# First query weights loaded third and used behind the second feature tile

## The chip, the cores and the metric

One core of a Trainium2 chip (trn2). The time is that of one launch in microseconds of device time, from three runs of each kernel. Engines, as the profile names them: PE (TensorE, matmuls), PEld (its weight loads), DVE (VectorE), ACT (ScalarE), POOL (GpSimd), SP (SyncE, which here issues nearly all loads). Each engine works through its own instructions in the order in which they stand; a semaphore holds an instruction until another engine, or a transfer, has got far enough.

## What is computed

A two-layer encoder on 512 frames of width 1024, in float32. Layer 0 is multi-head latent attention with a chunk mask and a SwiGLU feed-forward, layer 1 chunked attention over shared keys and values with another feed-forward. The change lies in the first 100 us, in the entry of layer 0:

```python
h = rms_norm(x, attn_pre_g[0])
a = h @ w_a                                   # 1024 -> 384 + 256 + 64
cq, ckv, kr = split(a, [384, 640])
q = (rms_norm(cq, g_q) @ w_uq)                # 8 heads: 128 plain + 64 rotary columns
kv = (rms_norm(ckv, g_kv) @ w_ukv)            # 8 heads: 128 key + 128 value columns
s = (q_nope k_nope^T + rope(q_rope) rope(k_rope)^T) * scale    # block-causal mask, softmax, p @ v, w_o
```

## The kernel before

Everything is kept transposed: features on 128 partitions, the 512 frames along the free side, so x is eight tiles `x[0]` to `x[7]` of 128x512. Each float32 operand is split into a high half, rounded to the format that PE multiplies, and the low rest: ACT writes the high half (`whi` of weights L144, `xh` of features L148, with the gain), DVE the rest (`wlo` L145, `xl` L149). `mm3` (L358) makes one product of three matmuls, high by high, high by low, low by high, each with 512 columns.

The norm's factor is not applied to x: the projection runs on x times the gain, and the factor of each frame is multiplied in later. So beside the projection ACT squares each x tile (L425, L428) and DVE adds the squares (L429, class `Sum`).

Weights come through `Feed`: a plan of tiles, added in order (L728 to L758); `load` issues a tile's DMA into one of 5 raw buffers, `split` makes `whi` and `wlo` in one of 3 buffers each, `next` hands out the next split tile, `ahead` splits one more early. The names in the profile: `in_w_akv` are the eight tiles of the 256 latent key/value and 64 rotary key columns (384 columns, one feature tile each), `in_w_aq` four tiles of the 384 query-latent columns (768 columns, two feature tiles each), then `in_w_uv` (values), `in_w_uqr` (rotary query), `in_w_qk` (a head's query and key).

`load_x` (L762) issues x tile k and then weight tile k. From the third on, POOL first writes one element of the new tile from an element of a tile two places earlier (L767, L286). That copy waits for the earlier tile's landing, and the DMA waits for the copy, so only some loads are under way at a time.

The loop L790 to L802 does, for each of the eight feature tiles: split the weights, split x, nine matmuls into three PSUM banks `b1` (three output tiles of three terms), issue the next loads, split the next weights ahead, square x. The four `in_w_aq` tiles follow in `proj` (L363), eighteen matmuls each into three banks `b2`, after the loop. Between its pieces (`some(rest, n)`) stand the sums of squares (`tot`, L438), the two factors by a power on POOL (L456), and their spreading over partitions on PE (`bc`, L473). Then the key/value latent is multiplied with its factor (L863) and split (`ckh`, `ckl`), and come the values `va` (L894), the rotary query (L908), the heads (L930) and attention, whose scores `sc` (L1013 to L1017) DVE turns into `p` (L498). The eight PSUM banks are four of tag `mm`, two `s`, two `t`: a matmul into a fresh bank waits until the bank's last reader is done.

The order on each engine is made by a scheduler from priorities (program order, which `first(n)` moves n places forward) and from its own estimate of durations; `issue_after` keeps an instruction behind another.

Of the kernel before, what the change touches and what calls it, by code (L numbers as in the profile page):

```python
# [11 lines left out]
F32R = mybir.dt.float32r  # L12
I32 = mybir.dt.int32
AF = mybir.ActivationFunctionType
OP = mybir.AluOpType
# [3 lines left out]
D, S, P = 1024, 512, 128  # L19
KT = D // P  # L20
# [48 lines left out]
def trunk(ctx: ExitStack, tc: tile.TileContext, a, out):  # L69
    nc = tc.nc  # L70
    V = nc.vector
# [10 lines left out]
    def name_(n):  # L82
        uid[0] += 1
        return f"{n}_{uid[0]}"

    def U(dt=F32, name="u"):
        return up.tile([P, S], dt, tag="u", name=name_(name), bufs=NU)
# [4 lines left out]
    def bank(tag="mm", name="b"):  # L92
        return ps.tile([P, S], F32, tag=tag, name=name_(name), bufs={"mm": 4, "s": 2, "t": 2}[tag])
# [29 lines left out]
    def g(n, k):  # L123
        return gains[:, n * KT + k:n * KT + k + 1]

    G_APRE, G_APOST, G_FPRE, G_FPOST = (0, 1), (2, 3), (4, 5), (6, 7)
# [8 lines left out]
    @contextmanager  # L135
    def first(n):

        tc.cur_priority -= n
        yield
        tc.cur_priority += n  # L140


    def split(dst_hi, dst_lo, src):
        return (nc.scalar.copy(dst_hi, src),  # L144
                V.tensor_tensor(dst_lo, src, dst_hi.bitcast(F32), op=OP.subtract))  # L145

    def split_scaled(dst_hi, dst_lo, src, col):
        return (nc.scalar.activation(dst_hi, src, AF.Copy, scale=col),  # L148
                V.scalar_tensor_tensor(dst_lo, src, col, dst_hi.bitcast(F32), op0=OP.mult, op1=OP.subtract))  # L149
# [202 lines left out]
    feed = Feed()  # L352
# [5 lines left out]
    def mm3(o, l, r, start, stop):  # L358
        nc.tensor.matmul(o, l[0], r[0], start=start, stop=False)  # L359
        nc.tensor.matmul(o, l[0], r[1], start=False, stop=False)  # L360
        nc.tensor.matmul(o, l[1], r[0], start=False, stop=stop)  # L361

    def proj(n_out, n_k, kc, rhs, banks, ahead=True):  # L363

        cols = n_out * P
        for c in range(0, n_k, kc):
            m = min(kc, n_k - c)
            w = feed.next(m * cols, ahead)
            for kk in range(m):
                if kk == 1:  # L370
                    feed.ahead()
                while len(rhs) <= c + kk:
                    yield False
                for j in range(n_out):
                    mm3(banks[j], w(kk * cols + j * P, P), rhs[c + kk], c + kk == 0, c + kk == n_k - 1)
                    yield True
# [82 lines left out]
    def rstd_of_scaled(ss, n, r0):  # L459

        v = small("v2")
        V.tensor_tensor(v, ss, r0, op=OP.mult)
        V.tensor_tensor(v, v, r0, op=OP.mult)
        r = rstd(v, n)
        o = small("r2")
        V.tensor_tensor(o, r, r0, op=OP.mult)
        return o
# [157 lines left out]
    def out_proj(rhs, n_k, post, have, n_last, late):  # L625
# [9 lines left out]
        for m in groups[:-n_last]:  # L635
            b = [bank() for _ in range(m)]
            weave(proj(m, n_k, KC[m], rhs, b))
            done.extend(b)
# [88 lines left out]

    for k in range(KT):  # L728
        feed.add(a["w_akv"][k], 384)
    for k in range(KT // 2):  # L730
        feed.add(a["w_aq"][k], 768)
    feed.add(a["w_uv"][0], 1024)
    feed.add(a["w_uqr"][0], 768)
# [26 lines left out]
    x = []  # L760

    def load_x():  # L762

        k = len(x)
        t = U(name="x")
        if k > 1:
            nc.gpsimd.tensor_copy(t[:1, :1], x[k - 2][:1, :1])  # L767
            feed.gate = feed.raw[k - 2]
        nc.sync.dma_start(t, a["x"][:, k])
        x.append(t)  # L770
        feed.load(k)
        feed.gate = None

    for k in range(4):
# [2 lines left out]
    def load_positions():  # L777
        for c in range(NQT):
            nc.sync.dma_start(pos_i[32 * c:32 * c + 32],
                            bass.AP(tensor=a["positions"].tensor, offset=a["positions"].offset + c * P,  # L780
                                    ap=[[0, 32], [1, P]]))
        nc.sync.dma_start(inv, a["inv_freq"])
# [4 lines left out]

    xs, sx = [], Sum()
    b1 = [bank() for _ in range(3)]
    for k in range(KT):  # L790
        h, l = U(F32R, "xh"), U(F32R, "xl")
        w = feed.next(384, False)
        feed.behind[k + 1] = split_scaled(h, l, x[k], g(G_APRE[0], k))
        xs.append((h, l))
        for j in range(3):
            mm3(b1[j], w(j * P, P), xs[k], k == 0, k == KT - 1)
        if len(x) < KT:
            load_x()
        feed.ahead()
        if k == 3:  # L800
            load_positions()
        sx.add(x[k])  # L802
    b2 = [bank("s"), bank("s"), bank()]
    rest = proj(3, KT, 2, xs, b2)
    skv = Sum()
    for j in range(2):
        skv.add(b1[j])
    ckv = []
# [8 lines left out]
    with first(100):  # L817
        rkv = rstd_of_scaled(ss, KVL, r0)
# [40 lines left out]
    rkv = spread(rkv)  # L859
    r0b = spread_sb(r0)  # L860
    cks = []
    for j in range(2):
        V.tensor_tensor(ckv[j], ckv[j], rkv, op=OP.mult)  # L863
        h, l = U(F32R, "ckh"), U(F32R, "ckl")
        feed.behind[13] = feed.behind[14] = split(h, l, ckv[j])
        cks.append((h, l))
    kr = U(name="kr")
    V.tensor_tensor(kr, b1[2], r0b, op=OP.mult)
# [5 lines left out]
    for j in range(3):  # L874
        h, l = U(F32R, "cqh"), U(F32R, "cql")
# [612 lines left out]
    x, sx = post.x, post.split  # L1488
    xs = sx.xs
# [20 lines left out]
    rest = v_half(0)  # L1510
# [137 lines left out]
    for kc in range(4):  # L1648
        w = feed.next(1024)
# [99 lines left out]
```

## Time and profile before

| | |
|---|---|
| runs | 1121.03, 1118.68, 1120.24 us; median 1120.24 |
| profiled execution | 1120.65 us, of which the span from first to last instruction is 1118.9 us |
| PE busy | 1102.8 us (99%) |
| DVE, ACT busy | 931.9 us (83%), 685.4 us (61%) |
| POOL busy | 70.4 us (6%) |
| granted TensorE clock, mean over the span | 0.999 |
| DMA | 150.85 MB, mean 135 GB/s |

PE is busy almost throughout, so a microsecond is won or lost only where PE waits. A matmul row's duration runs past the start of the next row, since matmuls are pipelined; the distance from start to start is what one costs.

### The profile page before, as it was taken

The numbers are of one execution on the slowest core, as the hardware profiler recorded it, in microseconds if no ns is written. First come the engines' busy times: TensorE is split into PE (matmuls) and PEld (weight loads), VectorE is DVE, ScalarE is ACT, GpSimd is POOL, SyncE is SP. The second block draws the span as 40 slices with busy tenths as digits, with TensorE's granted clock in tenths as the row PEclk, the third lists the DMA queues.
The fourth block names the chain that finished last, engine by engine and source line by source line (L and its number), as shares of the span: only waits on it lengthen the run. The fifth ranks groups of instructions, "written<-read, shape, count | busy, mean of one in ns | idle before, by whom it ended". The sixth has DMA issues, their size and how long they took to land.

```text
span 1118.9 us, 18985 instructions
## 1 busy us (share of the span) xinstructions
PE 1102.8 (99%) x6973; PEld 984.2 (88%) x6973; DVE 931.9 (83%) x1671; ACT 685.4 (61%) x1339; POOL 70.4 (6%) x106
## 2 busy tenths in 40 slices
PE   9999999999999999999999999999999999999997
PEld 6888889999999998888788888888999999998885
DVE  7788737999989889978858878657999899889977
ACT  6476637755555556668536777666755555566675
POOL 2200000000000002400100000000000000002402
PEclk9999999999999999999999999999999999999999
DMA  7333125323332448871456665534422322449923
GB/s 237 113 109 87 65 74 208 133 83 106 94 115 95 131 161 248 139 216 35 173 151 169 154 181 146 152 118 166 147 80 95 123 86 96 141 169 291 171 56 76
DMA packets 62991, 150.85 MB, mean 135 GB/s; under 512 B 8433, under 2 KB 10225, under 8 KB 62897
## 3 DMA queue, kind: packets, MB, share of 16 engines
q1 hardware_dynamic: 55552, 136.61, 38.6%
q0 software_dynamic: 6912, 12.59, 6.8%
q8 instruction: 55, 0.90, 0.3%
q10 hardware_dynamic: 432, 0.44, 0.1%
q14 instruction: 40, 0.32, 0.1%
HBM read 119.52 MB, written 9.63 MB: 115 GB/s over the span
## 4 chain that ended last, share of the span: by engine, by line
PE 84%; DVE 7%; DMA 3%; ACT 3%; issue 2%; POOL 1%; SPq 0%; POOLq 0%; DVEq 0%; ACTq 0%
PE al L1453 16%; PE b L359 10%; PE b L360 10%; PE b L361 10%; PE be L1453 8%; PE al L1203 8%; PE ga L1453 4%; PE be L1203 4%; PE de L1203 3%; PE ga L1203 3%; PE pt L512 2%; DVE wlo L145 2%; ACT whi L144 1%; DVE raw L174 1%; DMA raw<-in_w_pair 1%
## 5 line engine op out<-in xcount | busy, mean ns | idle before, releaser
L144 ACT CAST whi<-raw 128x1024 fp32r<-128x1024 f32 (+3 forms) x224 | 225.3, 1007 | 208.4 <-PE al L1453 74.0
L145 DVE TENSOR_TENSOR wlo<-raw,whi 128x1024 fp32r<-128x1024 f32 (+3 forms) x224 | 261.3, 1168 | 55.9 <-ACT whi L144 54.1
L1453 PE MATMUL al<-th,whi 128*128 128x256 f32 x432 | 122.8, 284 | 0.8 <-DVE ut L1465 0.8
L1453 PE MATMUL al<-th,wlo 128*128 128x256 f32 x432 | 121.1, 280 | 0.0
L1453 PE MATMUL al<-tl,whi 128*128 128x256 f32 x432 | 120.9, 280 | 0.0
L359 PE MATMUL b<-xh,whi 128*128 128x512 f32 (+1 forms) x304 | 117.3, 387 | 0.0
L360 PE MATMUL b<-xl,whi 128*128 128x512 f32 (+1 forms) x304 | 112.7, 371 | 0.2 <-DVE xl L149 0.2
L361 PE MATMUL b<-xh,wlo 128*128 128x512 f32 (+1 forms) x304 | 112.5, 370 | 0.0
L174 DVE TENSOR_TENSOR raw<-raw,raw 128x1024 f32<-128x1024 f32 x72 | 86.7, 1220 | 1.3 <-DMA raw<-in_w_pair 1.2
L1453 PEld LDWEIGHTS al<-th,whi 128*128 128x128 f32 x432 | 81.2, 188 | 3.2 <-DVE ut L1465 1.2
L1453 PEld LDWEIGHTS al<-th,wlo 128*128 128x128 f32 x432 | 81.3, 188 | 0.1
L1453 PEld LDWEIGHTS al<-tl,whi 128*128 128x128 f32 x432 | 81.3, 188 | 0.0
L500 ACT ACTIVATE p<-p,mn 128x128 f32<-128x128 f32 (+1 forms) x96 | 54.0, 562 | 39.5 <-DVE mn L498 38.4
L145 DVE TENSOR_TENSOR ptl<-pt,pth 128x128 fp32r<-128x128 f32 (+1 forms) x96 | 46.7, 486 | 29.4 <-ACT pth L144 23.7
L145 DVE TENSOR_TENSOR wlo<-wd,whi 128x512 fp32r<-128x512 f32 x86 | 56.7, 689 | 14.4 <-ACT whi L144 14.2
L361 PEld LDWEIGHTS b<-xh,wlo 128*128 128x128 f32 x304 | 57.5, 189 | 9.5
L144 ACT CAST whi<-wd 128x512 fp32r<-128x512 f32 x86 | 50.0, 618 | 25.5 <-PE al L1203 10.6
L359 PEld LDWEIGHTS b<-xh,whi 128*128 128x128 f32 x304 | 57.8, 190 | 7.1 <-ACT xh L148 0.7
L360 PEld LDWEIGHTS b<-xl,whi 128*128 128x128 f32 x304 | 57.8, 190 | 7.1 <-DVE xl L149 1.1
L144 ACT CAST pth<-pt 128x128 fp32r<-128x128 f32 (+1 forms) x96 | 40.3, 420 | 26.6 <-PE pt L512 25.7
L1203 PE MATMUL al<-whi,ph 128*128 128x512 f32 x132 | 51.8, 392 | 0.0
L1203 PE MATMUL al<-whi,pl 128*128 128x512 f32 x132 | 51.5, 390 | 0.0
(309 smaller groups left out, 3267.8 us busy)
## 6 DMA issues: line engine op xcount, KB each, us to landing
raw<-in_w_pair SPq DMA_DIRECT2D x72, 512.0 KB, 3.6
wd<-in_w_down SPq DMA_DIRECT2D x54, 256.0 KB, 5.7
raw<-in_w_o SPq DMA_DIRECT2D x16, 512.0 KB, 3.6
raw<-in_w_gu SPq DMA_DIRECT2D x16, 512.0 KB, 3.9
raw<-in_w_down SPq DMA_DIRECT2D x16, 512.0 KB, 4.3
raw<-in_w_qkb SPq DMA_DIRECT2D x16, 512.0 KB, 3.7
wd<-in_w_down POOLq DMA_DIRECT2D x22, 256.0 KB, 5.9
wd<-raw POOLq DMA_DIRECT2D x22, 256.0 KB, 4.4
```

The lines of the kernel that those rows point to most:

```text
L144: return (nc.scalar.copy(dst_hi, src), V.tensor_tensor(dst_lo, src, dst_hi.bitcast(F32), op=OP.subtract))
L145: V.tensor_tensor(dst_lo, src, dst_hi.bitcast(F32), op=OP.subtract))
L174: V.tensor_tensor(t, x, y, op=OP.add)
L359: nc.tensor.matmul(o, l[0], r[0], start=start, stop=False)
L360: nc.tensor.matmul(o, l[0], r[1], start=False, stop=False)
L361: nc.tensor.matmul(o, l[1], r[0], start=False, stop=stop)
L500: nc.scalar.activation(p[:, :n], p[:, :n], AF.Exp, bias=mn[:, :1], scale=-1.0, accum_out=self.sums[:, qt:qt + 1])
L512: nc.tensor.transpose(t[:, kt * P:(kt + 1) * P], p[:, kt * P:(kt + 1) * P], ident)
L1203: nc.tensor.matmul(to[e], l[c], r[d], start=j < 4 and k == 0 and n == 0, stop=k == NF // 2 - 1 and n == 2, skip_group_check=True)
L1453: nc.tensor.matmul(o, l[c], r[d], start=first_ and n == 0, stop=k == K2 - 1 and n == 2, skip_group_check=True)
```

## The change

The plan puts the first `in_w_aq` tile third, behind the second `in_w_akv` tile. `load_x` issues its DMA ahead of the third x tile, and later weight tiles one call later by index. In the loop x is split ahead of the weights (for all but the first tile), the matmuls of the first two feature tiles go term by term over the three banks instead of bank by bank, squares of x are taken one tile later, and behind the second feature tile the early query tile is used with both: eighteen matmuls, which `proj` then leaves out (`begun=2`). The multiplication and split of the key/value latent get priority 100.

```diff
--- before.py
+++ after.py
@@ -360,10 +360,10 @@
         nc.tensor.matmul(o, l[0], r[1], start=False, stop=False)
         nc.tensor.matmul(o, l[1], r[0], start=False, stop=stop)
 
-    def proj(n_out, n_k, kc, rhs, banks, ahead=True):
+    def proj(n_out, n_k, kc, rhs, banks, ahead=True, begun=0):
 
         cols = n_out * P
-        for c in range(0, n_k, kc):
+        for c in range(begun, n_k, kc):
             m = min(kc, n_k - c)
             w = feed.next(m * cols, ahead)
             for kk in range(m):
@@ -727,7 +727,9 @@
 
     for k in range(KT):
         feed.add(a["w_akv"][k], 384)
-    for k in range(KT // 2):
+        if k == 1:
+            feed.add(a["w_aq"][0], 768)
+    for k in range(1, KT // 2):
         feed.add(a["w_aq"][k], 768)
     feed.add(a["w_uv"][0], 1024)
     feed.add(a["w_uqr"][0], 768)
@@ -762,13 +764,16 @@
     def load_x():
 
         k = len(x)
+        if k == 2:
+            feed.gate = feed.raw[0]
+            feed.load(2)
         t = U(name="x")
         if k > 1:
             nc.gpsimd.tensor_copy(t[:1, :1], x[k - 2][:1, :1])
-            feed.gate = feed.raw[k - 2]
+            feed.gate = feed.raw[k - 1 if k > 3 else k - 2]
         nc.sync.dma_start(t, a["x"][:, k])
         x.append(t)
-        feed.load(k)
+        feed.load(k if k < 2 else k + 1)
         feed.gate = None
 
     for k in range(4):
@@ -787,21 +792,40 @@
 
     xs, sx = [], Sum()
     b1 = [bank() for _ in range(3)]
+    b2 = [bank("s"), bank("s"), bank()]
     for k in range(KT):
         h, l = U(F32R, "xh"), U(F32R, "xl")
-        w = feed.next(384, False)
-        feed.behind[k + 1] = split_scaled(h, l, x[k], g(G_APRE[0], k))
+        w = None if k else feed.next(384, False)
+        s = split_scaled(h, l, x[k], g(G_APRE[0], k))
+        if k:
+            feed.behind[feed.pos] = s
+            w = feed.next(384, False)
         xs.append((h, l))
-        for j in range(3):
-            mm3(b1[j], w(j * P, P), xs[k], k == 0, k == KT - 1)
+        if k < 2:
+
+            for n, (c, d) in enumerate(((0, 0), (0, 1), (1, 0)) if k else ((0, 0), (1, 0), (0, 1))):
+                for j in range(3):
+                    nc.tensor.matmul(b1[j], w(j * P, P)[c], xs[k][d], start=k + n == 0, stop=False)
+        else:
+            for j in range(3):
+                mm3(b1[j], w(j * P, P), xs[k], False, k == KT - 1)
         if len(x) < KT:
             load_x()
-        feed.ahead()
         if k == 3:
             load_positions()
-        sx.add(x[k])
-    b2 = [bank("s"), bank("s"), bank()]
-    rest = proj(3, KT, 2, xs, b2)
+        if k:
+            with ExitStack() as order:
+                for i in s if k < 3 else ():
+                    order.enter_context(tc.issue_after(i.ins))
+                sx.add(x[k - 1])
+        if k == 1:
+            w = feed.next(768, False)
+            for i in range(2):
+                for j in range(3):
+                    mm3(b2[j], w(i * 384 + j * P, P), xs[i], not i, False)
+    feed.ahead()
+    sx.add(x[-1])
+    rest = proj(3, KT, 2, xs, b2, begun=2)
     skv = Sum()
     for j in range(2):
         skv.add(b1[j])
@@ -860,9 +884,10 @@
     r0b = spread_sb(r0)
     cks = []
     for j in range(2):
-        V.tensor_tensor(ckv[j], ckv[j], rkv, op=OP.mult)
-        h, l = U(F32R, "ckh"), U(F32R, "ckl")
-        feed.behind[13] = feed.behind[14] = split(h, l, ckv[j])
+        with first(100):
+            V.tensor_tensor(ckv[j], ckv[j], rkv, op=OP.mult)
+            h, l = U(F32R, "ckh"), U(F32R, "ckl")
+            feed.behind[13] = feed.behind[14] = split(h, l, ckv[j])
         cks.append((h, l))
     kr = U(name="kr")
     V.tensor_tensor(kr, b1[2], r0b, op=OP.mult)
```

PE, the nine matmuls of the first feature tile and the first of the second (`b_` are the PSUM banks, the first x tile's halves are `xh_125`, `xl_126` before and `xh_131`, `xl_132` now). Before:

```order
L359 MATMUL b_122<-xh_125,whi_127 128x512
L360 MATMUL b_122<-xl_126,whi_127 128x512
L361 MATMUL b_122<-xh_125,wlo_128 128x512
L359 MATMUL b_123<-xh_125,whi_127 128x512
L360 MATMUL b_123<-xl_126,whi_127 128x512
L361 MATMUL b_123<-xh_125,wlo_128 128x512
L359 MATMUL b_124<-xh_125,whi_127 128x512
L360 MATMUL b_124<-xl_126,whi_127 128x512
L361 MATMUL b_124<-xh_125,wlo_128 128x512
L359 MATMUL b_122<-xh_154,whi_148 128x512
```

Now:

```order
L808 MATMUL b_125<-xh_131,whi_133 128x512
L808 MATMUL b_126<-xh_131,whi_133 128x512
L808 MATMUL b_127<-xh_131,whi_133 128x512
L808 MATMUL b_125<-xh_131,wlo_134 128x512
L808 MATMUL b_126<-xh_131,wlo_134 128x512
L808 MATMUL b_127<-xh_131,wlo_134 128x512
L808 MATMUL b_125<-xl_132,whi_133 128x512
L808 MATMUL b_126<-xl_132,whi_133 128x512
L808 MATMUL b_127<-xl_132,whi_133 128x512
L808 MATMUL b_125<-xh_154,whi_158 128x512
```

The low half of x was read by the second matmul and is now read by the seventh; the low half of the weights moved from the third to the fourth.

DVE, from the end of the first rotary product to the split of the first value tile of the second value half (`ra`, `rb` rotary products of the query, `rl` their low half, `r_` the query norm's factor from POOL, `va` values; L917 is L942 now, L915 and L916 are L940 and L941). Before:

```order
L917 TENSOR_TENSOR ra_643<-ra_643,rb_644 128x512
L452 TENSOR_SCALAR v_610<-v_131_607 128x4
L145 TENSOR_TENSOR wlo_772<-raw_695,whi_771 128x640
L466 TENSOR_TENSOR r_134_614<-r_612,r_356 128x4
L145 TENSOR_TENSOR rl_649<-ra_643,rh_648 128x512
L981 TENSOR_SCALAR nsq<-r_134_614 128x4
L145 TENSOR_TENSOR va_543<-b_720,va_543 128x512
```

Now:

```order
L452 TENSOR_SCALAR v_611<-v_131_608 128x4
L145 TENSOR_TENSOR wlo_733<-raw_626,whi_732 128x640
L466 TENSOR_TENSOR r_134_615<-r_613,r_381 128x4
L942 TENSOR_TENSOR ra_644<-ra_644,rb_645 128x512
L1006 TENSOR_SCALAR nsq<-r_134_615 128x4
L145 TENSOR_TENSOR rl_650<-ra_644,rh_649 128x512
L940 TENSOR_TENSOR ra_653<-b_618,sin_431 128x512
L941 TENSOR_TENSOR rb_654<-b_619,cos_432 128x512
L145 TENSOR_TENSOR wlo_773<-raw_696,whi_772 128x640
L145 TENSOR_TENSOR va_544<-b_721,va_544 128x512
```

The add into `ra` stands behind POOL's factor now, and two more rotary products and the weight split stand between `rl` and the value split.

ACT, around the key of the first head (`kh_706` before, `kh_707` now; `whi` 768 columns wide is the second rotary weight tile). Before:

```order
L144 CAST kh_706<-b_710 128x512
L144 CAST whi_838<-raw_729 128x640
L144 CAST qh_778<-b_762 128x512
L144 CAST whi_928<-raw_769 128x768
L144 CAST kh_780<-b_784 128x512
```

Now:

```order
L144 CAST whi_839<-raw_730 128x640
L144 CAST qh_705<-b_689 128x512
L144 CAST whi_929<-raw_770 128x768
L144 CAST kh_707<-b_711 128x512
L144 CAST qh_779<-b_763 128x512
L144 CAST kh_781<-b_785 128x512
```

The first head's key stood ahead of both weight casts and now stands behind the 768-column one; that cast takes the buffer of the second head's weights, and so waits until PE has read these for the last time, in both kernels.

## Rows read from the trace of the kernel before

**Rows 1.** The page's busy time of each engine: us, share, instructions.

```profile
PE 1102.8 (99%) x6973; PEld 984.2 (88%) x6973; DVE 931.9 (83%) x1671; ACT 685.4 (61%) x1339; POOL 70.4 (6%) x106
```

**Rows 2.** Stages: start:end length, busy us (instructions) per engine, granted clock, DMA share, GB/s.

```profile
5.00:11.00 6.00, 5.76 (x20) 4.08 (x20) 4.09 (x7) 4.04 (x8) 1.99 (x7) 1.00 0.78 224
...
31.50:60.00 28.50, 28.25 (x130) 22.68 (x128) 22.23 (x41) 14.75 (x26) 4.87 (x4) 1.00 0.40 112
60.00:75.00 15.00, 15.00 (x82) 12.87 (x83) 13.42 (x30) 13.30 (x29) 0.00 (x0) 1.00 0.49 136
```

**Rows 3.** PE in order of time: start, us, line, tiles, [idle before].

```profile
4.97 0.79 PE L359 MATMUL b<-xh,whi 128*128 128x512 f32 x1
5.76 0.79 PE L360 MATMUL b<-xl,whi 128*128 128x512 f32 x1
6.35 0.63 PE L361 MATMUL b<-xh,wlo 128*128 128x512 f32 x1
6.78 0.50 PE L359 MATMUL b<-xh,whi 128*128 128x512 f32 x1
7.12 0.39 PE L360 MATMUL b<-xl,whi 128*128 128x512 f32 x1
...
8.91 0.50 PE L360 MATMUL b<-xl,whi 128*128 128x512 f32 x1 [0.24 <-DVE xl L149]
...
10.85 0.40 PE L359 MATMUL b<-xh,whi 128*128 128x512 f32 x1
```

**Rows 4.** POOL, ACT, DVE at the start, in order of time.

```profile
5.95 0.17 POOL L767 COPY x<-x 1x1 f32<-1x1 f32 x1 [1.26 <-DMA x<-in_x]
...
6.41 0.51 ACT L144 CAST whi<-raw 128x384 fp32r<-128x384 f32 x1 [1.49 <-DMA raw<-in_w_akv]
...
7.36 0.71 ACT L148 ACTIVATE xh<-x,gains 128x512 fp32r<-128x512 f32 x1
...
8.10 0.75 DVE L149 SCALAR_TENSOR_TENSOR xl<-x,gains,xh 128x512 fp32r<-128x512 f32 x1 [0.59 <-ACT xh L148]
```

**Rows 5.** DMA issues of the first 40 us: count, size, us to landing.

```profile
raw<-in_w_aq SPq DMA_DIRECT2D x4, 384.0 KB, 4.8
```

**Rows 6.** PE, ACT and DVE around the end of the first projection.

```profile
24.50 0.60 PE L438 MATMUL tot<-ident,acc 128*128 128x128 f32 x4
...
30.68 0.39 PE L361 MATMUL b<-xh,wlo 128*128 128x512 f32 x1
31.23 1.06 PE L473 MATMUL bc<-ident,r 128*128 128x128 f32 x8 [0.17 <-DVE r L466]
...
21.85 0.84 ACT L144 CAST whi<-raw 128x768 fp32r<-128x768 f32 x1 [0.16 <-DMA raw<-in_w_aq]
...
23.70 0.69 DVE L429 TENSOR_TENSOR acc<-acc,sq 128x512 f32<-128x512 f32 x1
```

**Rows 7.** PE at the values of the latent, and DVE beside it.

```profile
41.66 0.39 PE L359 MATMUL b<-whi,ckh 128*128 128x512 f32 x1
...
58.17 0.50 PE L359 MATMUL b<-whi,ckh 128*128 128x512 f32 x1
...
59.97 0.50 PE L359 MATMUL b<-whi,ckh 128*128 128x512 f32 x1
...
57.44 0.68 DVE L145 TENSOR_TENSOR va<-b,va 128x512 fp32r<-128x512 f32 x1
58.04 0.68 DVE L915 TENSOR_TENSOR ra<-b,sin 128x512 f32<-128x512 f32 x1
```

**Rows 8.** POOL's power for the query norm.

```profile
55.46 1.01 POOL L456 TENSOR_TENSOR r<-v,mhalf 128x4 f32<-128x4 f32 x1 [9.02 <-DVE v L452]
```

**Rows 9.** ACT and DVE at the first scores.

```profile
65.02 0.83 ACT L144 CAST whi<-raw 128x768 fp32r<-128x768 f32 x1
65.76 0.58 ACT L144 CAST kh<-b 128x512 fp32r<-128x512 f32 x1
...
66.49 0.34 DVE L498 CUSTOM_DVE_ANT_0 p<-sc,mask,nsq 128x128 f32<-128x128 f32 x1
```

## The prediction

> **What bounds the kernel now.** The page's busy times come first: the reader is to see that PE is busy for 99% of the span and every other engine less [rows 1]. So time can move only where PE waits, or where it works slowly. The table by stages says where that is near the change: PE lacks 0.24 us of the stretch from 5 to 11 us, 0.25 us of 31.5 to 60, and nothing of 60 to 75 [rows 2]. The last is as important as the first: a wait that the change brings to that stretch is a pure loss. In 60 to 75 DVE and ACT are nearly full too (13.4 and 13.3 of 15 us) [rows 2], so a late split is not caught up at once. Then PE in order of time at the start. There one reads the distances from start to start: 0.43 us from 6.35 to 6.78, 0.34 to 7.12, and from 10.85 to 24.50 sixty matmuls at 13.65 / 60 = 0.2275 us [rows 3, 6]. The granted clock reads 1.00 in that stage [rows 2], but the distances are those of half and full rate, with the rise at about 7.0 us, after the bf16 matmuls that run from 1.2 us on and the first of the real ones. The first real matmul starts at 4.97, the nineteenth at 10.85 [rows 3], so the first two feature tiles cost 5.88 us.
>
> I reckon the difference against the profiled execution, 1120.65 us (span 1118.9 and 1.75 around it), and put it on the median of the three runs, 1120.24; the profiled one lies 0.4 above that. I call no change what stays within 0.2%, 2.2 us, since the three runs of this kernel spread by that much.
>
> **The first two tiles.** Before, the second matmul waits for the low half of x: 4.97 to 5.76. In the second tile it waits again, until 8.91 [rows 3], since on ACT the first square stands ahead of the split of x (that split starts at 7.36 although the tile is there at 5.95, and its weights are cast at 6.41) and DVE's low half follows at 8.10 [rows 4]. Now three matmuls run on the high halves, three on the low weights, and three on the low x, which DVE finishes by about 5.7. From 4.97 five matmuls at 0.43 reach 7.1, thirteen at 0.2275 reach 10.05. DVE's splits cost by columns: starts 0.6 apart for 512 [rows 7], so about 0.45 for 384, 0.9 for 768, 1.2 for 1024. Does the second tile's data come in time? x at 5.95, split 0.71 later at 6.66, weights cast by 7.1, low x (0.75) by 7.45, low weights by 8.0; the second tile starts at 8.0. Nothing waits. Gain: 10.85 - 10.05 = 0.8 us.
>
> Here the Trainium skill has a rule that could give another result (TensorE: Matmul & The Clock Gate, section What's actually happening): half rate is the default, activity lifts it, and the moment is not tied to the kernel's start. The rows agree as far as they go, with one rise near 7.0 us in one execution; what other executions do, none shows. It is priced with the rivals.
>
> **The early query tile.** Its 384 KB are issued once the first weights have landed; ACT's cast of these (0.51) and its split of x (0.71) end before 4.97 [rows 3, 4], so they are there by 3.7, and the load goes out by about 4.1. Such loads landed 4.8 us after issue in a crowded stretch [rows 5]: 8.9; then 0.84 on ACT [rows 6], 9.75, and 0.9 on DVE, 10.65. PE wants the high half at 10.05, the low one two matmuls on, at 10.5. By that long row it is 0.15 late, by a shorter landing it is there; I take 0. Eighteen matmuls there replace eighteen later at the same 0.2275: no change of work. They also give the loads of the third and later tiles 4.1 us more, so the 384 KB put ahead of them (some 1.7 us at the 224 GB/s of that stage [rows 2]) cost nothing.
>
> **The end of the projection.** Before, PE is through with a matmul at 30.68 + 0.23 = 30.91 and starts the spreading at 31.23: 0.3 us lost to DVE and POOL [rows 6]. That chain starts with DVE's sum of squares at 23.70, and the ACT squares before it are late because ACT still casts a query tile that landed late, at 21.85 [rows 6]. Now that load has about three microseconds more, ACT takes the squares as soon as the banks are done, some 0.4 us earlier by my reckoning. Gain: 0.3 us; at worst the wait stays.
>
> Then 24 matmuls instead of 42 stand between the spreading and the values of the latent. The chain in between (DVE: 1.2 for the low half of value weights, four small operations of about 0.3, two products 1.2, a low half behind its cast on ACT, and a second one: 0.6 each) is done some 5.5 us after the spreading begins; PE arrives after 0.8 + 5.5. The cover is 0.8 us, where before it was over 4. I cost it at nothing; if the chain slips by more than 0.8, the rest is lost.
>
> So the values start about 1.1 us earlier than at 41.66 [rows 7]. What follows is counted from there (V).
>
> **What the new order does to DVE, V+6 to V+20.** The sums of squares of the query latent moved forward on PE to V+6.35; DVE's second addition ends about V+6.4. Loss 0.1. Next the second half of the values. Its third tile takes the bank of the first, so it waits for DVE's split of that: before at 57.44, and PE goes on at 58.17 instead of 57.89; the fourth again, 59.97 instead of 59.69 [rows 7]. Together 0.56, and about 0.1 each for the slower restart. Now the DVE order around this place is another. DVE waits for POOL's power (1.01 us [rows 8]) with nothing beside it, since the add into the rotary product stands behind the factor, then 0.7 for ACT's cast of that product, which the weight split used to cover; then two more rotary products (0.6 each by the distance of 57.44 to 58.04 [rows 7]) and a weight split (640 columns, 0.75) stand ahead of the value split. Step by step: second product done V+11.0, power V+11.2 to V+12.25, add to V+13.0, cast to V+13.7, low half to V+14.4, products V+15.6, weights V+16.3, value split V+17.0. PE wants the bank at V+16.3. Loss 0.75 in place of the 0.28; the fourth tile then finds its bank free (0 in place of 0.28); the next head's first bank waits for another value split, behind a low half and a key copy, 0.3. With restarts the sum is 0.5 us more than before from V to the end of the second head's key (E).
>
> **The first head's key.** The ACT cast of the 768-column weights needs the buffer that PE reads until E; it starts right after, as before at 65.02, and the next cast follows 0.74 later, 0.58 long [rows 9]. The first head's key now is that next cast: ready at E+1.35. PE has three matmuls to do before it needs the key, 0.68. Loss 0.7. The key's low half stands behind that weight's low half on DVE and comes at E+2.45, PE wants it at E+2.2: 0.25. The third score tile needs a bank that DVE frees with its first score pass (0.34 [rows 9]), now behind two more head splits, 0.3. Loss together 1.25, in a stretch where PE lost nothing [rows 2]. Bounds: nothing, if ACT finds a gap that I do not see, and 2.0 with each of the three at half as much again.
>
> **Sum.** -0.8 - 0.3 + 0.5 + 1.25 = +0.65 us. The work is the same and the order behind 75 us is the same, so it carries to the end: 1120.24 + 0.65, **1120.9 us**: no change that can be measured, since the start's gain is given back at the rotary query and the first scores.
>
> **Rivals.** (a) The gain is kept: the later losses do not come, because ACT and DVE run further ahead of PE than I reckon (my times are sums of rows over 20 us; half a microsecond of slack undoes most of it). For it: PE waits little in 31.5 to 75 now [rows 2]; against it: both queues are strict in order and the waits are in the program. -1.1: 1119.1. If besides the clock rises at the first real matmul, as the denser start allows, the first tile takes 9 x 0.2275 and ends at 7.0; the second is then bound by its low weights at 8.0 and ends at 9.2, the query tile by its low half; 0.7 more: 1118.4. By the Trainium skill (TensorE: Matmul & The Clock Gate, What's actually happening) such a shift, either way, would be no surprise.
> (b) The early load collides. If the 16 DMA engines mix it with the second x and weight tile, under way at the same time, these land up to 1.7 us later (384 KB at 224 GB/s), the second tile starts at 9.0 and waits for its parts, and the 0.8 is gone; the rest stays: +1.5, 1121.7. Against: they are issued 2 us earlier on the same queue.
> (c) Slower. The new waits at the first scores let PE's clock fall, and the matmuls behind them run at 0.43 for as long as it took to rise at the start (1.2 to 7.0 us). That stretch holds 14 matmuls at 0.43, each 0.20 too slow: 2.8 more, 1123.7. It decides from the point where a wait is long enough. Against: before, the waits ahead of 58.17 and 59.97 end without it: from one to the other, six matmuls and the second wait take 1.80 [rows 7], where six at 0.43 alone would take 2.6. My longest new wait is 0.75.
>
> **How the numbers follow.** Forecast 0.48, (a) 0.30, (b) 0.13, (c) 0.09. Faster than 1118.0 needs (a) with the clock's help or a lucky median: 0.12. Slower than 1122.5 is (c), and a little of (b) and of the forecast's upper bound (2.0 for the scores in place of 1.25, and the 0.3 not won: +1.7): 0.11. The rest, 0.77, is no change. The range leaves out (c) and the far end of (a): 1118.0 to 1123.2. The likeliest case's own range is 1119.8 to 1122.3.
>
> **What would show it.** Right: the matmul after the early query tile's eighteen starts near 14.1; the spreading has no wait; the values start near 40.5; PE waits 0.7 for a value split 16 us later, and about 0.7 for ACT's key cast at the first score. Wrong: PE full through these two places (rival a); the second tile starting after 8.5 (b); distances of 0.43 after 60 us (c).

## The result, and the profile after

The changed kernel takes 1122.06 us (median of 13 runs, 1119.7 to 1123.26); the kernel before, on the same chip, 1120.11 (13 runs, 1117.8 to 1121.03). The ratio is 1.0016, 95% interval 1.0009 to 1.0024: 1.9 us, 0.17%, just inside what was called no change, and on its slow side. The profiled execution took 1121.3 us, span 1119.5.

The table by stages of the changed kernel, to be held against [rows 2]; the columns are the same.

```profile
5.00:11.00 6.00, 5.89 (x25) 4.57 (x26) 3.85 (x6) 4.09 (x8) 1.79 (x7) 1.00 0.88 284
31.50:60.00 28.50, 26.20 (x121) 21.18 (x120) 24.65 (x47) 14.59 (x27) 7.69 (x5) 1.00 0.43 114
60.00:75.00 15.00, 14.29 (x73) 11.14 (x72) 11.03 (x24) 11.17 (x24) 0.00 (x0) 1.00 0.43 126
```

PE gained 0.13 us in the first stage and lost 2.05 and 0.71 in the other two (28.25 and 15.00 before). The granted clock reads 1.00 in all three. Now PE in order of time; the loss at a wait is the distance between two starts less the 0.23 us of a matmul.

```profile
4.99 0.96 PE L808 MATMUL b<-xh,whi 128*128 128x512 f32 x3
5.79 0.85 PE L808 MATMUL b<-xh,wlo 128*128 128x512 f32 x3
...
9.42 0.39 PE L360 MATMUL b<-xl,whi 128*128 128x512 f32 x1
9.92 0.50 PE L361 MATMUL b<-xh,wlo 128*128 128x512 f32 x1
...
13.68 0.39 PE L359 MATMUL b<-xh,whi 128*128 128x512 f32 x1
...
33.67 1.03 PE L473 MATMUL bc<-ident,r 128*128 128x128 f32 x8
...
40.03 0.39 PE L359 MATMUL b<-whi,ckh 128*128 128x512 f32 x1
...
46.15 0.39 PE L359 MATMUL b<-cqh,whi 128*128 128x512 f32 x1
47.10 0.63 PE L438 MATMUL tot<-ident,acc 128*128 128x128 f32 x4 [0.56 <-DVE acc L429]
...
56.67 0.39 PE L361 MATMUL b<-whi,ckl 128*128 128x512 f32 x1
58.80 0.50 PE L359 MATMUL b<-whi,ckh 128*128 128x512 f32 x1 [1.74 <-DVE va L145]
...
65.96 0.39 PE L361 MATMUL b<-cqh,wlo 128*128 128x512 f32 x1
66.90 0.50 PE L1038 MATMUL sc<-kh,qh 128*128 128x128 f32 x2 [0.55 <-ACT kh L144]
...
75.96 0.60 PE L512 MATMUL pt<-ident,p 128*128 128x128 f32 x4
```

- Start [rows 3]: the third feature tile begins at 13.68, behind 36 matmuls. Before, it began at 10.85 behind eighteen; eighteen more at 0.2275 would have been at 14.95. So 1.27 us are gained, and the query tile's low weights cost 0.27 of wait (9.42 to 9.92) within that.
- The spreading at 33.67 has no wait any more; the values start at 40.03, 1.63 us earlier than at 41.66 [rows 6, 7].
- Then it is given back: 0.72 us ahead of the query norm (46.15 to 47.10), 1.90 for the third value tile (56.67 to 58.80), 0.71 for the first head's key (65.96 to 66.90); and, without rows here, 0.28 for the next head's bank and 0.29 at two places behind the key.
- The first transposition behind which the order of both kernels is the same starts at 75.96; before it started at 74.04 (the row below). The 1.92 us between them are close to the 1.95 between the medians. The two profiled executions end only 0.6 apart (spans 1119.5 and 1118.9), although PE's order between is the same, so the rows up to here account for the loss at this place, and the medians for the whole.

```profile
74.04 0.60 PE L512 MATMUL pt<-ident,p 128*128 128x128 f32 x4
```

Why two of the waits are longer than forecast stands in VectorE's and GpSimd's rows of that stretch.

```profile
45.17 0.68 DVE L145 TENSOR_TENSOR va<-b,va 128x512 fp32r<-128x512 f32 x1
45.77 1.18 DVE L429 TENSOR_TENSOR acc<-acc,sq 128x512 f32<-128x512 f32 x1
...
47.48 1.30 DVE L145 TENSOR_TENSOR wlo<-raw,whi 128x640 fp32r<-128x640 f32 x1
...
49.30 1.71 DVE L145 TENSOR_TENSOR wlo<-raw,whi 128x1024 fp32r<-128x1024 f32 x1
...
52.35 0.81 DVE L145 TENSOR_TENSOR wlo<-raw,whi 128x640 fp32r<-128x640 f32 x1
```

```profile
44.64 1.75 POOL L1011 TENSOR_TENSOR kr<-kr,cos 64x512 f32<-64x512 f32 x1 [11.39 <-DMA cos<-rot]
46.48 1.62 POOL L1010 TENSOR_TENSOR sik<-kr,sik 64x512 f32<-64x512 f32 x1
48.17 1.75 POOL L1012 TENSOR_TENSOR kr<-kr,sik 64x512 f32<-64x512 f32 x1
52.51 1.52 POOL L456 TENSOR_TENSOR r<-v,mhalf 128x4 f32<-128x4 f32 x1 [2.58 <-DVE v L452]
```

The accumulation (L429) took 0.69 in the kernel before [rows 6] and takes 1.18 here; a split of 640 columns 1.30, where the one at 52.35 takes 0.81. GpSimd's three products of the rotary key run beside them, and its power takes 1.52 where it took 1.01 [rows 8]. The value split at 45.17, which reads a bank of PSUM, has its 0.68 although a product stands beside it.

### The profile page after: what moved, and what is told of

It is laid out like the page before. It is cut to its first block, busy times and chain, and to the rows that moved or that the text cites. A ratio compares the mean times of both kernels' runs of the same rounds, so it can differ in the third digit from the quotient of the medians.

```text
span 1119.5 us, 18992 instructions
## 1 busy us (share of the span) xinstructions
PE 1102.1 (98%) x6973; PEld 983.6 (88%) x6973; DVE 932.7 (83%) x1671; ACT 685.2 (61%) x1339; POOL 74.4 (7%) x107
## 4 chain that ended last, share of the span: by engine, by line
PE 86%; DVE 6%; ACT 3%; DMA 3%; issue 2%; POOL 1%; SPq 0%; POOLq 0%; DVEq 0%; ACTq 0%
PE al L1478 17%; PE b L359 10%; PE b L360 10%; PE b L361 10%; PE be L1478 9%; PE al L1228 8%; PE ga L1478 4%; PE be L1228 4%; PE de L1228 3%; PE ga L1228 3%; PE pt L512 2%; DVE wlo L145 1%; ACT whi L144 1%; PE b L1633 1%; PE b L1632 1%
## 5 line engine op out<-in xcount | busy, mean ns | idle before, releaser
L144 ACT CAST whi<-raw 128x1024 fp32r<-128x1024 f32 (+2 forms) x224 | 225.2, 1007 | 206.1 <-PE al L1478 73.0
L145 DVE TENSOR_TENSOR wlo<-raw,whi 128x1024 fp32r<-128x1024 f32 (+2 forms) x224 | 262.4, 1173 | 56.7 <-ACT whi L144 53.1
L359 PE MATMUL b<-xh,whi 128*128 128x512 f32 (+1 forms) x298 | 114.5, 385 | 0.0
L361 PE MATMUL b<-xh,wlo 128*128 128x512 f32 (+1 forms) x298 | 110.1, 370 | 0.1
L360 PE MATMUL b<-xl,whi 128*128 128x512 f32 (+1 forms) x298 | 109.9, 369 | 0.0
```

What stands on the lines that cost most here:

```text
L144: return (nc.scalar.copy(dst_hi, src), V.tensor_tensor(dst_lo, src, dst_hi.bitcast(F32), op=OP.subtract))
```

## The experiments

The theory tested first: VectorE's operations with two operands in SBUF and GpSimd's operations keep each other out. Its rival: the new order of VectorE's queue alone makes the waits. Each ratio is against runs of the kernel before on the same chip.

**GpSimd's products cut to one column.** The other 511 columns of the key stay unrotated.

```
-  nc.gpsimd.tensor_tensor(sik[:64], kr[64:], sik[64:], op=OP.mult)
+  for n in (1,):
+      nc.gpsimd.tensor_tensor(sik[:64, :n], kr[64:, :n], sik[64:, :n], op=OP.mult)
   ... (and the two products behind it likewise)
```

> The changed kernel with GpSimd's three products of the rotary key cut from 512 columns to one (the rest of the key stays unrotated); the order on every engine is the changed kernel's. Theory: VectorE's operations on two SBUF operands and GpSimd's products hold each other up, about 0.5 us each. Then the accumulation takes 0.68 us and not 1.18, the two weight splits 0.82 and 1.22 and not 1.30 and 1.71; PE's wait ahead of the query norm falls from 0.72 us to 0.25 or less, the one for the value split from 1.9 to about 0.8; time about 1.5 us below the changed kernel, 1120.5, no different from the kernel before. Rival: VectorE's new order alone makes the wait, and the long operations are a symptom: both waits stay within 0.3 us of what they are, 1122.

1121.26 us, ratio 1.0001 (0.9992 to 1.0010). No instruction changed its place on any engine. VectorE, GpSimd and PE of this kernel:

```profile
46.01 0.68 DVE L429 TENSOR_TENSOR acc<-acc,sq 128x512 f32<-128x512 f32 x1
...
47.21 0.82 DVE L145 TENSOR_TENSOR wlo<-raw,whi 128x640 fp32r<-128x640 f32 x1
...
48.55 1.21 DVE L145 TENSOR_TENSOR wlo<-raw,whi 128x1024 fp32r<-128x1024 f32 x1
```

```profile
51.55 1.51 POOL L456 TENSOR_TENSOR r<-v,mhalf 128x4 f32<-128x4 f32 x1 [4.26 <-DVE v L452]
```

```profile
57.83 0.50 PE L359 MATMUL b<-whi,ckh 128*128 128x512 f32 x1 [1.04 <-DVE va L145]
```

The three operations have their 0.68, 0.82 and 1.21 us again. The wait ahead of the query norm is gone, that for the value split fell from 1.74 to 1.04 (the idle time in brackets). So the stretches were GpSimd's doing. They cost the changed kernel 1.2 us up to this matmul: it stands 18.77 us behind the start of the values there, 17.56 here (57.83 less 40.27). The power still takes 1.51: a weight split stands beside it here too. The rival falls for these 1.2 us; the 1.04 that stay come with the new order and the power. The timing alone would not separate this kernel from the changed one, whose second timing below is 1.0011 (1.0002 to 1.0020); the rows do.

**The products moved to an earlier phase.** With the angle and sine steps put ahead on VectorE by their priority, the sine tables land earlier.

```
+  with first(100):
       V.tensor_copy(pos, pos_i)
       ... (the steps up to the negated sine)
```

> The changed kernel with the angle and sine steps given priority on VectorE, so that the negated sine comes about 0.6 us earlier and with it the sine tables and GpSimd's first product (44.64 in the changed kernel, here about 44.0); the order on all other engines is the same. Theory: each product of GpSimd keeps VectorE's operation on two SBUF operands out until 0.1 us before its own end, and the other way round, so the loss hangs on the phase and earlier is not better: the first accumulation waits for the first product (ends about 45.8 in place of 45.25), the second for the second product (ends about 47.7 in place of 46.95); the wait ahead of the query norm grows from 0.7 us to about 1.4, total 0 to 1.5 us more than the changed kernel, 1121.5 to 1123. Rival: the products are late, and what counts is that they come earlier: the waits shrink by 0.5 us and more, 1121 or less.

1122.78 us, ratio 1.0016 (1.0008 to 1.0025); the changed kernel beside it had 1122.17 (1.0011, 1.0002 to 1.0020; below). VectorE, GpSimd and PE:

```profile
45.03 1.31 DVE L429 TENSOR_TENSOR acc<-acc,sq 128x512 f32<-128x512 f32 x1 [0.30 <-ACT sq L428]
...
46.87 1.34 DVE L429 TENSOR_TENSOR acc<-acc,sq 128x512 f32<-128x512 f32 x1
```

```profile
44.51 1.29 POOL L1012 TENSOR_TENSOR kr<-kr,cos 64x512 f32<-64x512 f32 x1 [10.71 <-DMA cos<-rot]
46.38 1.27 POOL L1011 TENSOR_TENSOR sik<-kr,sik 64x512 f32<-64x512 f32 x1 [0.59 <-DMA sik<-rot]
```

```profile
48.35 0.63 PE L438 MATMUL tot<-ident,acc 128*128 128x128 f32 x4 [1.34 <-DVE acc L429]
```

Against the start of the values the first product comes 0.6 us earlier (44.51 against 40.51; 44.64 against 40.03 in the changed kernel), and the wait ahead of the norm grows to 1.34, since now both accumulations meet a product that began first. The medians, 0.6 apart, don't tell this kernel from the changed one; the rows do. In both kernels a VectorE operation that was kept out ends a fixed time behind the end of GpSimd's: 46.34 - 45.80 = 0.54, 48.21 - 47.65 = 0.56 (accumulations), and in the changed kernel 46.95 - 46.39 = 0.56, 48.78 - 48.10 = 0.68 (640 columns), 51.01 - 49.92 = 1.09 (1024 columns): each its own undisturbed duration less 0.13. The other way round it is the same: the product at 46.48 ends 1.15 us behind the accumulation that ended at 46.95, alone it takes 1.28. So the later one waits for the whole of the earlier one, and doesn't run at half speed beside it. The Trainium skill says so (SBUF — State Buffer, section SBUF: two separate sides): VectorE with two SBUF inputs and a GpSimd operation that reads SBUF share a pair of ports as an exclusive lock for a whole instruction. The trace agrees for the products, in both directions. For the power it agrees only in one. In the changed kernel the power waits for the split at 52.35: it ends 0.87 behind that split's end, and alone it takes 1.01. In the kernel before, a weight split with two SBUF operands began 0.48 us behind the power [rows 8], and neither was kept out:

```profile
55.94 0.83 DVE L145 TENSOR_TENSOR wlo<-raw,whi 128x640 fp32r<-128x640 f32 x1 [0.57 <-ACT whi L144]
```

**The products on VectorE.**

```
-  nc.gpsimd.tensor_tensor(...)   three times
+  V.tensor_tensor(...)
```

> The changed kernel with the three products of the rotary key on VectorE in place of GpSimd (same arithmetic); the planner orders VectorE and ScalarE anew from there on. Theory of two engines that hold each other up: three operations of about 0.7 us are added to VectorE, but three stretches of 0.5 us go and the rest falls into the gaps in which it waits for GpSimd's power and ScalarE's cast (0.9 and 0.6 us), so the wait for the value split falls below 1.2 us and the key is no later: 1120.5 to 1121.3. Rival: VectorE is the bound of that stretch and 2.1 us more of work go straight into the wait: 1123 or more.

1120.31 us, ratio 0.9991 (0.9983 to 1.0000): 2.5 thousandths below the changed kernel's 1.0016, and as fast as the kernel before or a little faster.

```profile
50.71 1.01 POOL L456 TENSOR_TENSOR r<-v,mhalf 128x4 f32<-128x4 f32 x1 [17.45 <-DVE v L452]
```

```profile
57.51 0.50 PE L359 MATMUL b<-whi,ckh 128*128 128x512 f32 x1 [0.34 <-DVE va L145]
```

VectorE's operations there read PSUM while the power runs, and it takes 1.01 us again; the wait for the value split is 0.34. The planner also put the first head's key cast ahead of the 768-column cast here, so this kernel contains the gain of the key cast (tested alone below) too. At the transposition it stands at 73.73, 2.2 us ahead of the changed kernel's 75.96: as much as the 1.2 of the cut products and the 1.0 of the key cast together. More work on VectorE made it faster.

**The control on the kernel before.** The same edit there.

> The kernel before with the three products of the rotary key on VectorE in place of GpSimd, a control for the same edit on the changed kernel. Theory: in the kernel before GpSimd's products run while VectorE is idle or reads PSUM (1.28 us each, nothing stretched), so the edit has nothing to win and adds 2 us to a full VectorE: 0 to 1.5 us more than the kernel before, 1120.5 to 1122. Rival: the products are better on VectorE whatever stands beside them, and the gain on the changed kernel had nothing to do with the two engines holding each other up: 1119.5 or less.

1126.06 us, ratio 1.0059 (1.0045 to 1.0072): far above what I expected, though the rival, a gain everywhere, falls as well.

```profile
58.60 1.22 DVE L145 TENSOR_TENSOR wlo<-raw,whi 128x1024 fp32r<-128x1024 f32 x1
```

```profile
59.87 0.67 PE L360 MATMUL b<-wlo,ckh 128*128 128x512 f32 x1 [3.88 <-DVE wlo L145]
60.34 0.63 PE L361 MATMUL b<-whi,ckl 128*128 128x512 f32 x1
...
63.33 0.46 PE L360 MATMUL b<-wlo,ckh 128*128 128x512 f32 x1
```

The planner put the three products, the rest of the first rotary tile and two products of the next one ahead of the low half of the 1024-column weights, which ends only at 59.82, and PE waits 3.9 us for it. Then comes something that no wait of the changed kernel brought: from 60.34 to 63.33 seven matmuls stand 0.43 apart (2.99 us); the mean granted clock of 59.8 to 63.3 is 0.53. Wait and half rate together, 3.9 and 1.4 us, are nearly all of the 5.5 us that this kernel is behind at the transposition (79.55 against 74.04). So the control says that the edit is no gain by itself, but not what the products cost on VectorE.

**The key cast ahead.** The 768-column weights wait on ScalarE until the first head's key is cast.

```
+  s = split(kh, kl, bk)
+  if h == 0: feed.behind[19] = s[:1]
```

> The changed kernel with ScalarE's cast of the first head's key put ahead of the cast of the 768-column weights behind it; the planner then also moves one key matmul group and score matmuls of PE behind it. Theory: the 0.7 us wait for the key's high half and most of the 0.3 behind it go, with nothing in their place: 1.0 us less than the changed kernel, about 1121.0. Rival: ScalarE is full there, so what is put later waits instead (a score bank or the next head's key), and the time stays at 1122.

1121.61 us, ratio 1.0009 (1.0000 to 1.0018). The scores start at 65.50 and not at 66.90, without a wait; behind the group of scores and head matmuls that the planner shuffled 1.0 us is left (69.49 and 70.45 for the same matmul).

```profile
65.50 0.39 PE L1040 MATMUL sc<-kh,qh 128*128 128x128 f32 x2
```

As expected, by the rows: the timed interval overlaps the changed kernel's. This term of the forecast was near its size.

**Both mended in the changed kernel's own order.** The products on VectorE at lower priority, so that they fall into its waits, and the key cast ahead.

```
+  with first(-20):
-      nc.gpsimd.tensor_tensor(...)   three times
+      V.tensor_tensor(...)
   ... (the key cast as above)
```

> The changed kernel with both losses taken away in its own order: the rotary key's three products on VectorE behind more urgent work (into the gaps in which it waits for GpSimd's power and ScalarE's cast), and the first head's key cast ahead of the 768-column weights. Theory: the wait for the query norm falls to 0.2 us or less, that for the value split to 0.5 or less, the one for the key goes: 3 us less than the changed kernel, 1119.0 to 1119.5, at or just under the kernel before. Rival: VectorE is full, and the 2 us of products put in come back as a wait for a value split or for the key's low half: 1120.5 or more.

1120.57 us, ratio 0.9996 (0.9987 to 1.0005). The norm's and the key's waits are gone, the one for the value split is 0.94; the first product stands beside the power, which takes 1.51. I expected 0.5 at most, and 3 us less than the changed kernel, whose time on this chip is 1122.17: it is 1.6 less, where the rival put it. The start in this execution was also 0.6 us later, its half rate lasting to about 7 us.

**The start alone.** By terms and with x split ahead, in the kernel before, the query tile in its old place and the priority of the latent's multiplication left out. The first version let the second weights' cast slip ahead of the first split of x:

> The kernel before with the start alone: the first two tiles' matmuls by terms and the split of x ahead of weights and squares; the query tile stays in its old place, and the order behind the first feature tiles is that of the kernel before. Theory: the third to sixth tile follow their loads closely (ScalarE's casts of their weights wait for DMA until 14.6 us, and the low halves of x are done some 0.3 us ahead of their use), so without the early query tile between them the gain of the first two tiles is lost waiting for data: 0.3 to 0.4 us less than the kernel before, 1119.8. Rival: the gain of 1.3 us or more is made in the first two tiles alone and carried on: 1118.8 or less.

1122.72 us, ratio 1.0016 (1.0007 to 1.0025), and no answer: the first matmul waited until 7.24 for x.

```profile
7.24 1.21 PE L803 MATMUL b<-xh,whi 128*128 128x512 f32 x3 [2.38 <-ACT xh L148]
...
10.80 1.05 PE L803 MATMUL b<-xh,whi 128*128 128x512 f32 x3
```

Nine matmuls take 3.56 us from 7.24 to 10.80, where nine at full rate take 2.05: after 2.4 us without work they ran mostly at half rate (the mean granted clock of these 3.56 us is 0.58), and the third tile came at 13.05. The second version has the changed kernel's order of casts and splits for these tiles:

> The kernel before with the start alone, this time with the order of casts and splits that the changed kernel has for the first two tiles (the first split of x ahead of the second tile's weights). The query tile stays in its old place and the order behind the feature tiles is that of the kernel before. Theory: the first two tiles gain about 1.3 us, but the loads and casts of the third to sixth tile, which in the kernel before are done only 0.3 us ahead of their use, then end last and take most of it back: 0.3 to 0.6 us less than the kernel before, 1120.0. Rival: the loads have room, and the whole 1.3 us is carried to the end: 1119.2 or less.

1121.23 us, ratio 1.0016 (1.0007 to 1.0025): neither of the two expectations.

```profile
10.17 0.39 PE L359 MATMUL b<-xh,whi 128*128 128x512 f32 x1
...
22.90 0.50 PE L359 MATMUL b<-xh,whi 128*128 128x512 f32 x1 [0.33 <-ACT whi L144]
...
23.89 0.50 PE L361 MATMUL b<-xh,wlo 128*128 128x512 f32 x1 [0.26 <-DVE wlo L145]
...
32.24 0.95 PE L473 MATMUL bc<-ident,r 128*128 128x128 f32 x7 [0.78 <-DVE r L466]
```

```profile
22.01 0.83 ACT L144 CAST whi<-raw 128x768 fp32r<-128x768 f32 x1 [1.62 <-DMA raw<-in_w_aq]
```

The third feature tile starts 0.68 us earlier than in the kernel before, and no feature tile waits. The weights of the first query tile do: ScalarE waits 1.62 us for their load, PE 0.33 and 0.26, and the chain to the spreading is late by 0.78 more. At the spreading this kernel is 1.0 us behind the kernel before; what else the timed 1.8 us hold (0.8 to 2.8) the one profile doesn't show. So the dense start runs into the loads at the query tiles, not at the feature tiles.

**The early query tile alone.** The start of the kernel before, the tile loaded third and used behind the second feature tile; the priority of the latent's multiplication is left out here too. No run has that priority alone.

> The kernel before with the early query tile alone: loaded third, used behind the second feature tile; the first tiles' matmuls and splits in their old order. Behind the projection the order is the changed kernel's, but for one small operation on VectorE. Theory: all of the losses behind 40 us come with the early tile (24 in place of 42 matmuls between spreading and values, so GpSimd's products of the rotary key meet VectorE's operations on two SBUF operands) and none with the start: the spreading's wait (0.35) goes, some 3.3 us are lost between 46 and 70 us, and the start's gain is missing: 1123.0 to 1123.8, and the accumulation and the two weight splits behind it last 1.1 to 1.2, 1.3 and 1.7 us again. Rival: the losses come from the denser start, which leaves ScalarE and VectorE less time; with the old start they shrink by half or more: 1121.5 or less.

1123.24 us, ratio 1.0032 (1.0020 to 1.0045): as expected, so the losses come with the tile. They come at other operations than expected: both accumulations are stretched, and the 1024-column split keeps its 1.21.

```profile
45.68 1.71 DVE L429 TENSOR_TENSOR acc<-acc,sq 128x512 f32<-128x512 f32 x1 [0.30 <-ACT sq L428]
...
47.91 1.49 DVE L429 TENSOR_TENSOR acc<-acc,sq 128x512 f32<-128x512 f32 x1
```

```profile
45.56 1.28 POOL L999 TENSOR_TENSOR kr<-kr,cos 64x512 f32<-64x512 f32 x1 [11.18 <-DMA cos<-rot]
47.58 1.27 POOL L998 TENSOR_TENSOR sik<-kr,sik 64x512 f32<-64x512 f32 x1 [0.74 <-DMA sik<-rot]
```

```profile
49.55 0.63 PE L438 MATMUL tot<-ident,acc 128*128 128x128 f32 x4 [1.89 <-DVE acc L429]
...
50.70 0.56 PE L360 MATMUL b<-cql,whi 128*128 128x512 f32 x1
...
54.05 0.46 PE L359 MATMUL b<-cqh,whi 128*128 128x512 f32 x1
```

Here both accumulations meet a product that has just begun, at the worst phase: 1.71 and 1.49 us. PE waits 1.89, takes up work at 49.55 at full rate, falls to half at about 50.7 and is back at 54; the mean granted clock of 50.7 to 54.0 is 0.51, the 1.2 GHz level. Eight matmuls take 3.35 us from 50.70 to 54.05, where eight at 0.2275 take 1.82: 1.5 us that the changed kernel did not lose. So with the tile the changed start is worth 1.6 thousandths (1.0032 to 1.0016); without the tile it costs as much (1.0016). In this profiled execution the kernel is 3.3 us behind the changed one at the transposition (79.29 against 75.96): 1.1 of them at the start of the values (41.16 against 40.03), 2.2 by phase and clock. But the execution is 1.9 us slower than this kernel's median (1125.14 against 1123.24, five runs), so how the timed 1.6 thousandths divide is not shown.

**The changed kernel once more.**

> The changed kernel once more, beside the two above on the same chip: 1.5 to 2 us more than the kernel before. Its profile shows whether the long accumulation (1.18 us) and weight splits (1.30 and 1.71) and the waits of 0.7, 1.9 and 0.7 us come again, which by both theories they do, and at which matmul the clock rises at the start.

1122.17 us, ratio 1.0011 (1.0002 to 1.0020): 1.2 us, a little less than expected. The rows are those of the first profile: accumulation 1.19, weight splits 1.30 and 1.70, waits of 0.6, 1.7 and 0.5 by the profile. At the start the first three matmuls take 0.84 from start to start, so the clock rose at about 5.3 us again; in the profiles of other kernels with this same start it rose at about 6 or 7.

## Why the prediction was right, and where its terms were not

The call, no change that can be measured and the gain given back at the rotary query and the first scores, was right; the time, 1120.9 against 1122.06, was too low by 1.2 us. The call held with 0.3 us to spare (1.95 of 2.2): the start gained 0.5 more than forecast and the stretch behind lost 1.8 more, and that the first took part of the second back was luck.

- **The first two tiles**, 0.8 forecast, 1.27 measured. The clock rose with the first real matmuls, as rival (a) had it in part, the second tile ended at 9.2, and the query tile waited 0.27 for its low half. With the rise at about 7, as in the kernel with both mended, the second tile ends at 10.05, the forecast's figure: the 0.47 more is the clock of the profiled execution, and other executions had less of it.
- **The early query tile** came nearly in time, as forecast: issued at 3.64, cast at 8.04, its low half 0.27 late. It did not delay x (second split at 5.59), so rival (b) fell. What I had not seen is that it carries the start: without it the gain is more than lost.
- **The spreading**: 0.3 forecast, 0.35 measured, and the cover of 0.8 behind it held.
- **The new order on VectorE** is the step that failed in size: +0.5 forecast, +2.3 measured (0.72 + 1.90 + 0.28, less the 0.56 of before). The value split, forecast for V+17.0, ended at V+18.7 (58.06 + 0.69, less 40.03). I gave every operation the duration it had in the kernel before and left out that GpSimd's products, which there ran while VectorE was idle or read PSUM, would now stand beside sums and weight splits from SBUF. That is 0.5 us three times, and a fourth time at the power. The rule of the Trainium skill named above speaks of this, and I did not weigh it. Cutting the products took 1.2 us of it away. What stayed is a loss of 1.20 (56.40 to 57.83) at the third value tile. By size it is the 0.75 forecast and the power's 0.5, but no run frees the power alone and keeps the rest.
- **The first head's key**: 1.25 forecast, 1.0 measured, for the reason given; the key cast put ahead took it away.
- **Rival (c)** was not what happened, but its mechanism exists: after 1.89 and 3.9 us of wait in two other kernels the clock fell, for 3.3 and at least 3.0 us. In the changed kernel PE waited 1.74 at 58.80 and kept full rate.

The sum by measured terms is -1.63 + 2.3 + 1.0 = 1.7, the traces show 1.92. The 0.2 between are not assigned. From there to the end the order is the same; the two profiles drift by 1.3 us against each other there (1.92 apart, then 0.6), so only the medians speak for the whole.

## What to carry to other kernels

When a change moves work between engines' queues, a duration from the old trace holds only while the same neighbours stand beside it: list for each moved VectorE operation what GpSimd does at that time and whether both read SBUF. A gain at the start is worth what the next loads and the next shared resource let through, so forecast the phase of the stretches behind it and not their order alone. Work that an engine does "for free" on GpSimd can be cheaper on VectorE itself when it falls into a wait; the same edit cost the kernel before 6.5 us, where it pushed back a weight split.

## What the runs showed of the hardware that was not expected

- GpSimd's 64x512 product and VectorE's two-operand SBUF operations exclude each other whole, in either direction; the one kept out ends its own duration less 0.13 us behind the other. An accumulation of 0.68 us took up to 1.71, and a value split that reads PSUM kept its 0.68. The short power (128x4) is kept out in the same way when VectorE's operation began first, but did not keep out a split that began 0.48 us behind it.
- TensorE's fall to half rate was seen behind the wait, not in it: work resumed at 49.55 with a granted clock of 1.00, the rate fell at about 50.7 and was back at 54. One wait of 1.74 us passed without it, one of 1.89 did not.
- With the same start the rate rose at about 5.3, 6 or 7 us in the profiles of different kernels; the third group of matmuls started at 6.48 or at 7.33. This is read from the distances of the matmuls (0.43 or 0.23 us), since the granted clock reads 1.00 at the start in all of them.
